# A hybrid gMLP / state-space layer on one core: block sums moved ahead, dt's place among the gates, layer norm of v behind the scan

## Chip, core and metric

The kernel runs on one core of a Trainium2 chip. Five engines run side by side, each through its own queue of instructions in order: TensorE (PE, matmuls and transposes), VectorE (DVE), ScalarE (ACT), GpSimd (POOL) and SyncE (SP, which here only issues DMAs). The metric is the device time of one execution in microseconds. The kernel before took 2279.49 us in the median of three runs (2277.6 to 2282.93).

## The reference

One layer (DEPTH is 1) works on T = 1024 prompt tokens and 64 sample tokens of width 1024, all in fp32. Cut to what matters:

```
h = rms_norm(x, pre_mix_w)
u, v, z, xbc, dt_raw, g_a, g_b = split(h @ w_in)          # 1024 -> u 1024, v 1024, z 2048, xbc 3072, dt 32, gates 2 x 1024
u = gelu(u)
v = layer_norm(gelu(v), gmlp_ln_w, gmlp_ln_b)             # v of the sample rows is an output
o_a = u * gmlp_spatial(v, gmlp_ws, gmlp_bs)               # per group a 128 x 128 mix over positions
xbc, conv_state = causal_conv(xbc, ...)                   # width 4, silu
dt = softplus(dt_raw + dt_bias);  a = -exp(a_log)
y, h_last = ssd(xs, dt, a, B, C, h0)                      # state-space scan, 4 groups of 8 heads
o_b = gated_group_rms_norm(y + d_skip * xs, z, ssm_norm_w)
x = x + rms_norm((sigmoid(g_a) * (o_a @ w_branch_a) + sigmoid(g_b) * (o_b @ w_branch_b)) @ w_out)
x = x + rms_norm(relu(rms_norm(x) @ w_up)^2 @ w_down)
```

## The kernel before

Tokens lie in tiles: tiles 0 to 7 are prompt rows of 128, tile 8 holds the 64 sample rows. Every fp32 matrix is split into a high and a low part (ACT writes the high part, line 81; DVE or POOL subtracts for the low one, line 82), and a product takes three matmuls: high by high, low by high, high by low. A weight block is loaded into a buffer "raw", of which there are two in the whole kernel, and split from there into "wh" and "wl".

A scheduler puts the instructions of each engine into an order from the program, with its own estimate of when each can start; at run time an engine takes them in that order. A buffer of a pool can be written again when its last reader is done, and a pool that opens over the space of a closed one waits in the same way.

The stages around the change, in program order:

1. *z, lower columns.* h is normalised tile by tile, transposed and split (first, first_T). Two halves of z's lower 1024 columns follow, each with four weight quarters (wM, lines 102 to 110) and a loop over the nine tiles (z_tile). Beside the second half, sums() makes block sums of h (operands e4, e5, e6) on POOL and DVE.
2. *v and z's upper columns by seven products.* Each is a 2 x 2 block product with seven products instead of eight, in the order P2, P1, P6, P5, P7, P3, P4, first for v (b = 0), then for z (b = 1). build() (line 352) loads weight pieces and adds them up on POOL for the product after next, prep() splits them for the next one. The pool "pm" of this stage opens over the space of stage 1. sum_e1 (line 481) makes one more block sum, E1, four times: two additions on POOL, a subtraction on DVE and a split. In the loop over products these four are popped from a list at every odd m, from the first product on.
3. *gates.* gate_gen (line 570) is a generator of 48 projections of 24 matmuls; each next() does one. Three stand before the scan's pool "ssd" opens, 5 behind the scan and 4 behind u; the others lie inside the scan.
4. *dt, scan operands and scan.* dt_part (line 199) is a generator: dt's weights and matmuls, then the softplus chain on DVE and ACT, then two cumulative sums on PE (lines 254 and 257) and their transposes. For each of four groups (gi) the operands B, C and x are projected, passed through the convolution (xbc_chunk) and the scan runs tile by tile (stage_a, stage_b, stage_c) on three big buffers "xs" of 128 x 1536.
5. *Layer norm of v.* v_d holds gelu(v) in DRAM. ln_gen (line 656) normalises it tile by tile in place: load two halves, sum, centre, square, scale, store. It is stepped once for each third of a projection of x, and twice behind each group's scan; it has two half buffers "ln".
6. *u and the spatial mix*, then o_a @ w_branch_a with the gates, and what follows. The transposes of the norm's weight and bias (lnr, line 876) stand ahead of the first spatial mix.

The layer norm's step in the projection loop and the rest of it are:

```
                for q in range(4):
                    for t, th in xbc_chunk(gi * 4 + q, lambda t: sp.tile([P, 384], F32, tag="th", bufs=3, name="th")):
                        next(lng, None)
                        ...
            for _ in range(5):
                next(gates)
            for _ in lng:
                pass
```

Of the kernel before, what the change touches and what calls it, by code (L numbers as in the profile page):

```python
# [8 lines left out]
F32 = mybir.dt.float32  # L9
# [6 lines left out]
P = 128  # L16
D = 1024
# [29 lines left out]
def program(tc, a):  # L47
# [3 lines left out]
    with ctx:  # L51
# [32 lines left out]
        def wunit(src, shape, lo_eng=None, pool=None):  # L84
# [3 lines left out]
            raw = wpool.tile([P, 1024], F32, tag="raw", bufs=2, name="raw")  # L88
# [13 lines left out]
        def wM_gen(w, c0, lo_eng=None, pool=None):  # L102

            pool = pool or [None] * 4
            for j in range(4):
                src = w[j * 256:(j + 1) * 256, c0:c0 + 512].rearrange("(k p) n -> p k n", p=P)
                yield wunit(src, (2, 512), lo_eng, pool[j])
# [244 lines left out]
        def build(k, q):  # L352
# [4 lines left out]
            base = k > 1  # L357
# [33 lines left out]
        with tc.tile_pool(name="p0", bufs=1, side="right") as p0:  # L391
# [81 lines left out]

        with tc.tile_pool(name="pm", bufs=1, side="right") as pm, tc.tile_pool(name="xp1", bufs=3, space=PSUM) as xp:
# [31 lines left out]
            for k, (b, n) in enumerate(plan):  # L506
# [12 lines left out]
                for m in range(4):  # L519
# [61 lines left out]
        for _ in range(3):  # L581
            next(gates)
        first_w = [wT(w_in, OFF_X + (16 + gi) * P) for gi in range(1)]
        u_w = []
        with tc.tile_pool(name="ssd", bufs=1, side="right") as sp, \
# [11 lines left out]
            tp = tpp.tile([P, 4, P], F32, tag="tp", name="tp")  # L597
            pe.transpose(tp[:, 0, :120], crow[:120, 0, :], ident[:120, :120])
            pe.transpose(tp[:, 1, :72], crow[:72, 1, :], ident[:72, :72])
            v.tensor_scalar(out=cw, in0=tp[:, 0, :120], scalar1=0.5, scalar2=None, op0=ALU.mult)  # L600
            v.tensor_copy(hist.rearrange("p w c -> p (w c)"), tp[:, 1, :72])

# [53 lines left out]
            def ln_gen():  # L656

                def half(name):
                    return sp.tile([P, 512], F32, tag="ln", bufs=2, name=name)

                for i in (8, 0, 1, 2, 3, 4, 5, 6, 7):
                    R = ROWS[i]
                    hs_ = [half("la"), half("lb")]
                    for f in range(2):
                        nc.sync.dma_start(out=hs_[f][:R], in_=v_d[i * P:i * P + R, f * 512:f * 512 + 512])
                    yield
                    m = sp.tile([P, 8], F32, tag="lm", bufs=2, name="lm")
                    for f in range(2):
                        v.tensor_reduce(out=m[:R, f:f + 1], in_=hs_[f][:R], axis=mybir.AxisListType.X, op=ALU.add)
                    g.tensor_tensor(out=m[:R, 2:3], in0=m[:R, 0:1], in1=m[:R, 1:2], op=ALU.add)  # L670
                    g.tensor_scalar(out=m[:R, 2:3], in0=m[:R, 2:3], scalar1=-1.0 / D, scalar2=None, op0=ALU.mult)
                    yield
                    for f in range(2):
                        s.activation(hs_[f][:R], hs_[f][:R], AF.Identity, bias=m[:R, 2:3])
                    yield
                    jk = sp.tile([P, 4, P], F32, tag="s4", bufs=1, name="jk").rearrange("p a b -> p (a b)")
                    for f in range(2):
                        s.activation(jk[:R], hs_[f][:R], AF.Square, accum_out=m[:R, 3 + f:4 + f])
                    g.tensor_tensor(out=m[:R, 5:6], in0=m[:R, 3:4], in1=m[:R, 4:5], op=ALU.add)
                    r = rsq(sp, m[:, 5:6], R, D, 4 * EPS)  # L680
                    yield
                    for f in range(2):
                        v.tensor_scalar(out=hs_[f][:R], in0=hs_[f][:R], scalar1=r[:R], scalar2=None, op0=ALU.mult)
                        nc.sync.dma_start(out=v_d[i * P:i * P + R, f * 512:f * 512 + 512], in_=hs_[f][:R])
                    if i == 8:
                        yield
                        for f in range(2):
                            x = hs_[f]
                            o = sp.tile([P, 4, P], F32, tag="s4", bufs=1, name="lo").rearrange("p a b -> p (a b)")
                            for name, op in (("gmlp_ln_w", ALU.mult), ("gmlp_ln_b", ALU.add)):  # L690
                                nc.sync.dma_start(out=o[:R], in_=a[name][0, f * 512:f * 512 + 512].partition_broadcast(R))
                                v.tensor_tensor(out=x[:R], in0=x[:R], in1=o[:R], op=op)
                            g.dma_start(out=a["new_gmlp_v_sample"][0, 0][:, f * 512:f * 512 + 512], in_=x[:R])
                        yield
# [3 lines left out]
            dtg = dt_part(wa, wb_, wc, wd)  # L698
            next(dtg)
# [901 lines left out]
```

## Time and profile before

| what | number |
|---|---|
| median of three runs | 2279.49 us |
| the profiled execution | 2282.59 us, of which the span from first to last instruction is 2280.5 |
| PE busy with matmuls | 2173.4 us, 95% of the span |
| PE weight loads, beside matmuls | 1954.6 us, 86% |
| DVE, ACT, POOL busy | 1426.2 (63%), 967.3 (42%), 901.0 us (40%) |
| mean granted clock of TensorE | 0.982 of full speed |

PE is the engine that sets the time: in 40 slices of the span it is below 90% in only a few, most of them early. Matmuls are pipelined, so a listed duration is longer than the step from one to the next. A row of a timeline reads: start and duration in us, engine, line, operation, output and inputs, shape and count, and in brackets the idle time of that engine before it and what ended it. SPq, ACTq and POOLq are DMA issues. A row of windows reads: the stretch, its length in us, then the busy time (and count) of PE, PE's weight loads, DVE, ACT and POOL, the granted clock as a share of full speed, the share of the DMA engines' time and GB/s; its sum row adds the windows up (546 to 609, 711 to 771, and the two that are shown).

### The profile page before, as it was taken

The page shows a single profiled execution, that of the slowest core. Times are in us where ns is not written, and L with a number is a line of the kernel's source. Part 1 is how long each engine was busy: PE and PEld are TensorE (multiplying, and loading weights), DVE is VectorE, ACT ScalarE, POOL GpSimd, SP SyncE. Part 2 cuts the span into 40 slices and gives each one's busy share as a digit, 9 for nine tenths or more (in the row PEclk, how much of TensorE's full clock was granted, in tenths as well). Part 3 has the DMA queues.
Part 4 walks back from the last instruction along what each step waited for, and adds up shares of the span by engine and source line. Part 5 has one row for each costly group of instructions (what it writes and reads, how often), then busy time and mean ns, then how long its engine had stood idle before and what let it go on. Part 6 is the DMA issues. An engine that isn't in the chain of part 4 may idle for free.

```text
span 2280.5 us, 33458 instructions
## 1 busy us (share of the span) xinstructions
PE 2173.4 (95%) x12547; PEld 1954.6 (86%) x12547; DVE 1426.2 (63%) x1972; ACT 967.3 (42%) x1875; POOL 901.0 (40%) x861
## 2 busy tenths in 40 slices
PE   8979997999999999999999999998999998999997
PEld 6767777978889879989999999777999997788785
DVE  5667646676677676665732247377555556577777
ACT  5225435446455545433321123245555554433333
POOL 3455521374473572662221455353222223122134
PEclk9999998999999999999999999999999999999999
DMA  6245662153344352342253535443445457534543
GB/s 206 87 130 190 191 191 77 53 148 109 116 140 123 99 137 75 109 141 75 79 189 91 168 114 170 148 155 117 146 152 154 130 159 242 162 110 135 171 121 111
DMA packets 332939, 309.15 MB, mean 136 GB/s; under 512 B 41499, under 2 KB 286957, under 8 KB 332265
## 3 DMA queue, kind: packets, MB, share of 16 engines
q1 hardware_dynamic: 300648, 268.77, 39.4%
q10 hardware_dynamic: 27152, 22.29, 2.9%
q0 software_dynamic: 4976, 15.95, 1.9%
q8 instruction: 99, 1.62, 0.3%
q14 instruction: 64, 0.52, 0.1%
HBM read 224.68 MB, written 81.49 MB: 134 GB/s over the span
## 4 chain that ended last, share of the span: by engine, by line
PE 64%; DVE 9%; POOL 8%; DMA 8%; issue 8%; ACT 3%; SPq 0%; ACTq 0%; POOLq 0%; DVEq 0%
PE ps L120 7%; PE ps L119 7%; PE ps L121 7%; PE X L1233 3%; PE X L1231 3%; PE X L1232 3%; PE X L1382 3%; PE X L1383 3%; PE X L1381 2%; PE ps L1381 2%; PE ps L1382 2%; PE ps L1383 2%; PE ps L971 2%; PE ps L970 2%; PE ps L969 2%
## 5 line engine op out<-in xcount | busy, mean ns | idle before, releaser
L119 PE MATMUL ps<-hTh,wh 128*128 128x384 f32 (+1 forms) x1152 | 387.0, 336 | 0.0
L120 PE MATMUL ps<-hTl,wh 128*128 128x384 f32 (+1 forms) x1152 | 385.3, 334 | 0.0
L121 PE MATMUL ps<-hTh,wl 128*128 128x384 f32 (+1 forms) x1152 | 384.7, 334 | 0.0
L82 POOL TENSOR_TENSOR wl<-raw,wh 128x1024 fp32r<-128x1024 f32 x74 | 181.9, 2460 | 249.7 <-ACT wh L81 241.2
L81 ACT ACTIVATE wh<-raw 128x1024 fp32r<-128x1024 f32 x112 | 118.4, 1057 | 254.6 <-PE ps L120 98.5
L120 PEld LDWEIGHTS ps<-hTl,wh 128*128 128x128 f32 x1152 | 217.6, 189 | 8.8 <-issue 8.1
L119 PEld LDWEIGHTS ps<-hTh,wh 128*128 128x128 f32 x1152 | 217.6, 189 | 8.0 <-issue 7.4
L121 PEld LDWEIGHTS ps<-hTh,wl 128*128 128x128 f32 x1152 | 217.5, 189 | 6.4 <-issue 6.3
L1231 PE MATMUL X<-hb,wu 128*128 128x272 f32 x512 | 147.9, 290 | 1.5 <-ACT ev L1238 1.0
L627 DVE SCALAR_TENSOR_TENSOR acc<-raw,cw,acc 128x384 f32<-128x384 f32 (+1 forms) x216 | 132.8, 616 | 25.1 <-ACT acc L625 20.6
L1232 PE MATMUL X<-hb,wu 128*128 128x272 f32 x512 | 147.7, 289 | 0.0
L1233 PE MATMUL X<-hb,wu 128*128 128x272 f32 x512 | 146.4, 290 | 0.0
L1375 POOL TENSOR_TENSOR wd<-wd,wd 128x1024 f32<-128x1024 f32 x32 | 85.4, 2672 | 113.2 <-DVE dl L82 74.8
L759 ACT ACTIVATE bc<-bc,pcum 128x128 f32<-128x128 f32 (+1 forms) x288 | 90.6, 384 | 85.9 <-POOL bc L756 83.4
L970 PE MATMUL ps<-ob,wh 128*128 128x384 f32 (+1 forms) x384 | 125.4, 327 | 0.0
L971 PE MATMUL ps<-ob,wl 128*128 128x384 f32 (+1 forms) x384 | 125.4, 327 | 0.0
L969 PE MATMUL ps<-ob,wh 128*128 128x384 f32 (+1 forms) x384 | 125.4, 326 | 0.0
L81 ACT ACTIVATE dh<-wd 128x1024 fp32r<-128x1024 f32 x56 | 59.1, 1055 | 153.6 <-PE ps L1382 79.6
L82 DVE TENSOR_TENSOR dl<-xd,dh 128x1024 fp32r<-128x1024 f32 x56 | 100.5, 1820 | 4.0 <-DMA rs_d<-C 2.5
L82 DVE TENSOR_TENSOR dl<-wd,dh 128x1024 fp32r<-128x1024 f32 x56 | 72.0, 1292 | 48.9 <-ACT dh L81 47.2
L1382 PE MATMUL X<-dl,dh 128*128 128x512 f32 x256 | 100.4, 395 | 0.0
L1383 PE MATMUL X<-dh,dl 128*128 128x512 f32 x256 | 100.3, 394 | 0.0
(447 smaller groups left out, 6047.4 us busy)
## 6 DMA issues: line engine op xcount, KB each, us to landing
raw<-w_in SPq DMA_DIRECT2D x56, 512.0 KB, 4.0
xd<-rc_d SPq DMA_DIRECT2D x112, 256.0 KB, 4.0
rc_d<-E SPq DMA_DIRECT2D x32, 544.0 KB, 3.5
bc<-ac_d SPq DMA_DIRECT2D x64, 256.0 KB, 4.0
raw<-w_branch_b SPq DMA_DIRECT2D x32, 512.0 KB, 3.8
wr<-w_up SPq DMA_DIRECT2D x32, 512.0 KB, 4.1
wd<-w_down SPq DMA_DIRECT2D x16, 1024.0 KB, 5.8
w<-w_in SPq DMA_DIRECT2D x28, 512.0 KB, 4.1
```

What stands on the lines that cost most here:

```text
L81: s.activation(hi, src, AF.Copy)
L82: (lo_eng or v).tensor_tensor(out=lo, in0=src, in1=hi, op=ALU.subtract)
L119: pe.matmul(ps[:, :n], wh[:, k, :], hh[:, k, :n], start=(k == 0), stop=False)
L120: pe.matmul(ps[:, :n], wh[:, k, :], hl[:, k, :n], start=False, stop=False)
L121: pe.matmul(ps[:, :n], wl[:, k, :], hh[:, k, :n], start=False, stop=(k == 7))
L969: pe.matmul(ps[:, :n], wh[:, k, :], ob[:, kk, :], start=(k == 0), stop=False)
L970: pe.matmul(ps[:, :n], wh[:, k, :], ob[:, 4 + kk, :], start=False, stop=False)
L1231: pe.matmul(ps, wh[:, k, :], bh[:, k, :], start=start and k == 0, stop=False, skip_group_check=chain)
L1232: pe.matmul(ps, wh[:, k, :], bl[:, k, :], start=False, stop=False, skip_group_check=chain)
L1233: pe.matmul(ps, wl[:, k, :], bh[:, k, :], start=False, stop=k == 3, skip_group_check=chain)
L1382: pe.matmul(ps, xh, wl, start=False, stop=False, skip_group_check=chain)
L1383: pe.matmul(ps, xl, wh, start=False, stop=q == 3, skip_group_check=chain)
```

## The change

It has four parts.

- *z, second half:* two of the four weight quarters are loaded into two "xt" buffers of stage 1 instead of the two "raw" ones, and the sample tile goes first in the loop over tiles.
- *E1 and the pieces of w11:* for P1, as before for the later products, the pieces come into buffers "k4" of the pool "pm" instead of "raw". The second addition of E1 goes from POOL to DVE, and the four steps are popped at P1's m = 3 and P6's m = 0, 1, 2.
- *dt:* one gate projection, dt's matmuls, one gate, the rest of dt's softplus, one gate, and then the transposes of the convolution's weights, instead of three gates, those transposes and dt. In the loop over B's projection dt's generator is stepped at the last third only.
- *Layer norm of v:* ln_gen handles one whole tile, in one of the three "xs" buffers, and runs behind the last scan, three tiles at a time, with the nine remaining gates between; none are left behind u.

```diff
-            ws = wM(w_in, OFF_Z + 512, pool=[(p0, 1)] + [None] * 3)
+            ws = wM(w_in, OFF_Z + 512, pool=[(p0, 1)] + [None] * 3, raws=[None] * 2 + [lambda: p0.tile([P, D], F32, tag="xt", bufs=2, name="raw")] * 2)
...
-            for i in range(NT):
+            for i in (8, 0, 1, 2, 3, 4, 5, 6, 7):
                 z_tile(ws, 1, i)
...
-            base = k > 1
+            base = k > 0
...
-                for x, i in ((x12, 4 + m), (x11, m)):
-                    g.tensor_tensor(out=x, in0=row_op(i, 0, 0), in1=row_op(i, 0, 1), op=ALU.add)
+                for x, i, e in ((x12, 4 + m, g), (x11, m, v)):
+                    e.tensor_tensor(out=x, in0=row_op(i, 0, 0), in1=row_op(i, 0, 1), op=ALU.add)
...
-                        if todo:
-                            todo.pop(0)()
+                    if todo and (k == 1 and m == 3 or k == 2 and m < 3):
+                        todo.pop(0)()
...
-        for _ in range(3):
-            next(gates)
...
+            def ln_gen(i):
+
+                R = ROWS[i]
+                w = sp.tile([P, 3, 512], F32, tag="xs", bufs=3, name="lnw").rearrange("p a b -> p (a b)")
+                x, jk = w[:R, 0:D], w[:R, D:D + 512]
+                nc.sync.dma_start(out=x, in_=v_d[i * P:i * P + R, :])
...
+                yield
+                yield
+                m = sp.tile([P, 8], F32, tag="lm", bufs=4, name="lm")
+                v.tensor_reduce(out=m[:R, 0:1], in_=x, axis=mybir.AxisListType.X, op=ALU.add)
+                g.tensor_scalar(out=m[:R, 2:3], in0=m[:R, 0:1], scalar1=-1.0 / D, scalar2=None, op0=ALU.mult)
+                yield
+                s.activation(x, x, AF.Identity, bias=m[:R, 2:3])
+                yield
+                for f in range(2):
+                    s.activation(jk, x[:, f * 512:f * 512 + 512], AF.Square, accum_out=m[:R, 3 + f:4 + f])
+                g.tensor_tensor(out=m[:R, 5:6], in0=m[:R, 3:4], in1=m[:R, 4:5], op=ALU.add)
+                r = rsq(sp, m[:, 5:6], R, D, 4 * EPS)
+                yield
+                v.tensor_scalar(out=x, in0=x, scalar1=r[:R], scalar2=None, op0=ALU.mult)
+                nc.sync.dma_start(out=v_d[i * P:i * P + R, :], in_=x)
...
+            next(gates)
             next(dtg)
-            lng = ln_gen()
+            next(gates)
+            next(dtg)
+            next(gates)
...
-                    next(dtg, None)
+                    if t == 2:
+                        next(dtg, None)
...
-                        next(lng, None)
...
-                next(lng, None)
-                next(lng, None)
-            for _ in range(5):
-                next(gates)
-            for _ in lng:
-                pass
+
+            live, left = [], [ln_gen(i) for i in (8, 0, 1, 2, 3, 4, 5, 6, 7)]
+            turn = 0
+            while live or left:
+                while left and len(live) < 3:
+                    live.append(left.pop(0))
+                live = [x for x in live if next(x, True) is None]
+                turn += 1
+                if turn % 2 == 0:
+                    next(gates, None)
```

POOL's order at the start of stage 2, before. Lines 365 and 367 add up P6's two weight pieces (v2, one of each line per piece), line 485 makes E1's block sums, line 316 is part of v's gelu, line 321 a store.

```order
L316 TENSOR_SCALAR t_1118<-t_1118 128x512
L367 TENSOR_TENSOR v2_1030<-v2_1030,w12_1035 128x1024
L316 TENSOR_SCALAR t_1150<-t_1150 128x512
L485 TENSOR_TENSOR x_1088<-hTh1_96,hTl1_97 128x512
L485 TENSOR_TENSOR x_1087<-hTh0_94,hTl0_95 128x512
L321 DMA v_d_81<-cz_1015 128x512
L365 TENSOR_TENSOR v2_1079<-v2_1079,w11_1081 128x1024
L485 TENSOR_TENSOR x_1143<-hTh2_98,hTl2_99 128x512
L321 DMA v_d_81<-cz_1045 128x512
L485 TENSOR_TENSOR x_1142<-hTh0_94,hTl0_95 128x512
```

In this piece the second weight piece, v2_1079, has only its first addition. The same place with the change:

```order
L431 DMA z_d_80<-sz_962 128x512
L365 TENSOR_TENSOR v2_1030<-v2_1030,w11_1032 128x1024
L367 TENSOR_TENSOR v2_1030<-v2_1030,w12_1035 128x1024
L485 TENSOR_TENSOR x_1178<-hTh1_96,hTl1_97 128x512
L365 TENSOR_TENSOR v2_1072<-v2_1072,w11_1074 128x1024
L367 TENSOR_TENSOR v2_1072<-v2_1072,w12_1077 128x1024
L316 TENSOR_SCALAR t_1104<-t_1104 128x512
L316 TENSOR_SCALAR t_1129<-t_1129 128x512
```

Both pieces now stand directly behind z's last store (line 431), with one block sum between them.

SP's order of DMA issues around the load of the norm's weights (lnr), before. raw is a weight load, sz a tile of z and bc a block of decays for the scan, bs belongs to the spatial mix, vc is the first reload of the normalised v.

```order
L746 DMA sz_9156<-z_d_80 128x512
L755 DMA bc_9268<-ac_d_83 128x4x128
L746 DMA sz_9254<-z_d_80 128x512
L90 DMA raw_10021<-w_in 128x8x128
L90 DMA raw_10167<-w_in 128x8x128
L870 DMA lnr_9617<-gmlp_ln_w 8x128
L871 DMA lnr_9617<-gmlp_ln_b 8x128
L185 DMA bs_9724<-gmlp_bs 128x128
```

And with the change (lines 653 and 673 are the norm's loads and stores, each name lnw_... one tile):

```order
L673 DMA v_d_81<-lnw_9354 128x1024
L673 DMA v_d_81<-lnw_9401 128x1024
L653 DMA lnw_9489<-v_d_81 128x1024
L673 DMA v_d_81<-lnw_9487 128x1024
L653 DMA lnw_9533<-v_d_81 128x1024
L90 DMA raw_10503<-w_in 128x8x128
L673 DMA v_d_81<-lnw_9489 128x1024
L673 DMA v_d_81<-lnw_9533 128x1024
L871 DMA lnr_9661<-gmlp_ln_w 8x128
L872 DMA lnr_9661<-gmlp_ln_b 8x128
L185 DMA bs_9768<-gmlp_bs 128x128
```

These are the norm's last four tiles (4 to 7; the store of tile 3 opens the piece, that of tile 4 is the second row). The load of tile 7, lnw_9533, follows the store of tile 4, lnw_9401, whose buffer it takes; the load of the norm's weights follows the last tile's store.

## Rows read from the trace of the kernel before

**Rows 1.** PE's timeline, second half of z (start, us, engine, line, operation)

```profile
75.59 0.50 PE L134 MATMUL ps<-wl,hTh 128*128 128x512 f32 x1 [3.09 <-DVE wl L82]
...
78.27 0.63 PE L135 MATMUL ps<-wh,hTl 128*128 128x512 f32 x1
...
80.74 0.39 PE L133 MATMUL ps<-wh,hTh 128*128 128x512 f32 x1
...
92.58 0.50 PE L133 MATMUL ps<-wh,hTh 128*128 128x512 f32 x1 [1.88 <-DVE sz L430]
```

**Rows 2.** PE's timeline, product P6 of v

```profile
158.41 0.80 PE L493 MATMUL X<-wh,e4h 128*128 128x512 f32 x1 [3.67 <-DVE cz L532]
...
172.83 2.07 PE L493 MATMUL X<-wh,e4h 128*128 128x512 f32 x4 [9.95 <-ACT wh L81]
```

**Rows 3.** POOL's timeline, P6's weight pieces and block sums

```profile
141.46 2.40 POOL L365 TENSOR_TENSOR v<-v,w 128x1024 f32<-128x1024 f32 x1 [1.24 <-DMA v<-w_in]
...
157.85 2.96 POOL L485 TENSOR_TENSOR x<-hTh,hTl 128x512 f32<-128x512 f32 x2
...
163.47 2.79 POOL L367 TENSOR_TENSOR v<-v,w 128x1024 f32<-128x1024 f32 x1
```

**Rows 4.** Timelines of SP and PE, dt's weights, matmuls and cumulative sum

```profile
323.04 0.34 SPq L185 DMA_DIRECT2D dskip<-d_skip  x1
...
325.69 0.43 SPq L213 DMA_DIRECT2D wd<-w_in  x1
...
330.39 0.36 PE L219 MATMUL ps<-hTh,wd 128*32 128x384 f32 x1 [2.41 <-ACT wd L81]
...
369.35 1.30 PE L254 MATMUL ps<-wb__2427,wa 128*128 128x288 f32 x2 [14.14 <-DVE wb__2427 L250]
```

**Rows 5.** Windows: projections without the norm, scan's end to u's end, sum of four

```profile
872.00:936.00 64.00, 64.00 (x405) 63.51 (x404) 42.71 (x76) 33.18 (x74) 14.59 (x18) 1.00 0.21 56
1018.00:1156.00 138.00, 138.00 (x878) 136.16 (x877) 85.14 (x165) 46.11 (x88) 36.80 (x36) 1.00 0.32 92
sum 325.00, PE 319.59 PEld 314.69 DVE 214.18 ACT 153.59 POOL 91.29; mean PE 79.90 PEld 78.67 DVE 53.55 ACT 38.40 POOL 22.82
```

**Rows 6.** E1's sums by their tile: ns min/median/max, first and last start

```profile
L486 DVE TENSOR_TENSOR x<-x x4: 693/1132/4273, 140.2 to 166.7; 128x512 f32<-128x512 f32 x4
```

**Rows 7.** Timelines of POOL and PE, scan's end

```profile
1011.01 1.29 POOL L796 TENSOR_TENSOR y<-y,xs 128x512 f32<-128x512 f32 x1 [2.06 <-DVE y L795]
...
1017.55 0.60 PE L650 MATMUL tp<-ident,S 128*128 128x128 f32 x4
...
1032.03 0.23 PE L876 MATMUL tp<-ident,lnr 16*128 16x16 f32 x1
```

**Rows 8.** DMA issues: count, KB each, median us to landing

```profile
la<-v_d SPq DMA_DIRECT2D x6, 256.0 KB, 2.7
...
v_d<-la SPq DMA_DIRECT2D x7, 256.0 KB, 2.1
...
vc<-v_d SPq DMA_DIRECT2D x8, 512.0 KB, 4.2
```

**Rows 9.** Lines, layer norm: busy us, mean ns of one | idle before

```profile
L143 POOL TENSOR_TENSOR rs<-rs,pw 128x1 f32<-128x1 f32 (+1 forms) x45 | 27.0, 601 | 2.7
...
L674 ACT ACTIVATE la<-la,lm 128x512 f32<-128x512 f32 (+1 forms) x9 | 6.5, 721 | 19.4 <-POOL lm L671 17.8 <-POOL raw L611 1.6
...
L669 DVE TENSOR_REDUCE lm<-la 128x1 f32<-128x512 f32 (+1 forms) x9 | 6.2, 685 | 12.7 <-DMA la<-v_d 12.7
...
L678 ACT ACTIVATE jk<-la 128x512 f32<-128x512 f32 (+1 forms) x9 | 5.6, 623 | 0.6 <-DMA new_ssm_prompt<-s 0.6
...
L683 DVE TENSOR_SCALAR la<-la,rs 128x512 f32<-128x512 f32 (+1 forms) x9 | 4.4, 488 | 8.0 <-POOL rs L143 8.0
```

**Rows 10.** SP's timeline, one tile of the layer norm

```profile
716.13 0.46 SPq L665 DMA_DIRECT2D la<-v_d  x1
...
732.74 0.32 SPq L684 DMA_DIRECT2D v_d<-la  x1
```

More of the change, by code (lines that the diff above doesn't have):

```diff
@@ L82, in split, with wunit @@
             (lo_eng or v).tensor_tensor(out=lo, in0=src, in1=hi, op=ALU.subtract)
-        def wunit(src, shape, lo_eng=None, pool=None):
+        def wunit(src, shape, lo_eng=None, pool=None, raw=None):
             pool, nb = pool or (wpool, 4)
             m = shape[0] * shape[1]
-            raw = wpool.tile([P, 1024], F32, tag="raw", bufs=2, name="raw")
+            raw = raw() if raw else wpool.tile([P, 1024], F32, tag="raw", bufs=2, name="raw")
             r3 = raw[:, :m].rearrange("p (a b) -> p a b", a=shape[0])
@@ L100, in wT, with wM_gen @@
             return wunit(src, (8, P), lo_eng)
-        def wM_gen(w, c0, lo_eng=None, pool=None):
-            pool = pool or [None] * 4
+        def wM_gen(w, c0, lo_eng=None, pool=None, raws=None):
+            pool, raws = pool or [None] * 4, raws or [None] * 4
             for j in range(4):
                 src = w[j * 256:(j + 1) * 256, c0:c0 + 512].rearrange("(k p) n -> p k n", p=P)
-                yield wunit(src, (2, 512), lo_eng, pool[j])
+                yield wunit(src, (2, 512), lo_eng, pool[j], raws[j])
         def wM(*args, **kw):
@@ L596, in program @@
             nc.sync.dma_start(out=crow[0:72, 1, :], in_=a["cache_conv"][0, 0].rearrange("w (c p) -> (w c) p", p=P))
[L597 to L601, printed above, removed]
             def xbc_chunk(c, out):
@@ L654, in hbc @@
                 return x.unsqueeze(2).to_broadcast([R, HG, HD])
[L656 to L665, printed above, removed]
-                    yield
[L667 to L671, printed above, removed]
-                    yield
[L673 to L694, printed above, removed]
@@ new lines, in ln_gen @@
+            def ln_gen(i):
[3 more added lines that the diff above has]
+                nc.sync.dma_start(out=x, in_=v_d[i * P:i * P + R, :])
+                if i == 8:
+                    wb8 = sp.tile([P, 3, 512], F32, tag="xs", bufs=3, name="lnb")[:R]
+                    names = [("gmlp_ln_w", 0), ("gmlp_ln_b", 0), ("gmlp_ln_w", 1), ("gmlp_ln_b", 1)]
+                    for k, (name, f) in enumerate(names[:3]):
+                        nc.sync.dma_start(out=wb8[:, k, :], in_=a[name][0, f * 512:f * 512 + 512].partition_broadcast(R))
+                yield
[13 more added lines that the diff above has]
+                nc.sync.dma_start(out=v_d[i * P:i * P + R, :], in_=x)
+                if i == 8:
+                    nc.sync.dma_start(out=jk, in_=a["gmlp_ln_b"][0, 512:1024].partition_broadcast(R))
+                    yield
+                    yield
+                    for k, (name, f) in enumerate(names):
+                        xf = x[:, f * 512:f * 512 + 512]
+                        v.tensor_tensor(out=xf, in0=xf, in1=wb8[:, k, :] if k < 3 else jk, op=ALU.mult if k % 2 == 0 else ALU.add)
+                    g.dma_start(out=a["new_gmlp_v_sample"][0, 0], in_=x)
@@ L698, in program @@
             dtg = dt_part(wa, wb_, wc, wd)
+            next(gates)
             next(dtg)
-            lng = ln_gen()
+            next(gates)
+            next(dtg)
+            next(gates)
+            tp = tpp.tile([P, 4, P], F32, tag="tp", name="tp")
+            pe.transpose(tp[:, 0, :120], crow[:120, 0, :], ident[:120, :120])
+            pe.transpose(tp[:, 1, :72], crow[:72, 1, :], ident[:72, :72])
+            v.tensor_scalar(out=cw, in0=tp[:, 0, :120], scalar1=0.5, scalar2=None, op0=ALU.mult)
+            v.tensor_copy(hist.rearrange("p w c -> p (w c)"), tp[:, 1, :72])
             for gi in range(G):
```

## The prediction

> **What bounds the kernel now.** I read the page first. By its first part, in the table above, PE has matmuls running for 2173 of 2280.5 us, so only the 107 us in which it runs nothing, and the stretches in which it runs at half speed, are to be had. The change adds and drops next to no matmuls. Everything is therefore a question of where PE waits, and I went through PE's waits from the longest down and asked of each whether the change touches it; the timeline of PE gave their places. In the second half of z's projection PE waits 3.09 us for a weight split and 1.88 us for a finished z tile, and after each the matmuls run at half speed for a while (0.63 us long where they are 0.39 later) [rows 1]. In product P6 it waits 3.67 and 9.95 us [rows 2], the second time for weights that POOL has to add up first: POOL's pieces of that weight begin at 141.46 and end at 166.26, with block sums between them [rows 3]. At dt it waits 2.41 us for dt's weights and 14.14 us for the softplus chain [rows 4]. In the projections of the scan's first operands PE is idle 5.4 us over the two windows in which the layer norm runs beside them (the sum of the four windows less their two gapless rows), and not at all in the window without it; nor from the scan's end to the end of u [rows 5]. The waits inside the scan, some 16 us in all, are not touched.
>
> **The change part by part.** The sum is made against the profiled execution, 2282.59 us, which lies 3.1 us above the median of the runs, 2279.49.
>
> *z, second half.* Two of four weight quarters get buffers of their own and are loaded early, and the block sums no longer stand on DVE ahead of the splits. That takes the 3.09 and the 1.88 us and two half-speed stretches of eight matmuls each, 16 x 0.24 = 3.8: 8.8 at most. Nothing else is queued between the splits, but the sums now all lie in this half, with their DVE and POOL work (block adds, splits) beside z's. Bounds 0 to 8.8; I take 6, near the upper end, since only the engine order could give it back.
>
> *P6.* In the new order POOL's two weight pieces follow the opening with one block add between them instead of six and some gelu work: 2 x 2.4 + 2 x 2.8 + 1.5, about 12 us from the first load's arrival, where it took 24.8 [rows 3]. PE needs them 26 us after z's end and has them after 22 to 26. Also the buffers of this block come free behind the last prompt tile of z, not behind the sample tile (which now goes first), so the block's loads go out some 6 us sooner. Gone: 3.67 + 9.95 idle [rows 2] and twenty half-speed matmuls, 4.8: 18.4 at most. What is late next: P1's pieces of w11 now use a buffer of the new block and cannot be loaded before it opens; they are split some 12 us after z's end, when PE wants them. Bounds 5 to 18.4, value 15. By the Trainium skill (SBUF — State Buffer, "Who interferes with whom") a DVE instruction with two SBUF inputs and a GpSimd instruction that reads SBUF exclude each other, so a block add moved from POOL to DVE would still hold POOL up; the four DVE subtractions beside POOL's adds took 0.69 to 4.27 us here, which agrees [rows 6]. By that rule the term would be some 2 us smaller.
>
> *dt.* One gate projection instead of three stands ahead of dt's matmuls. 82 PE instructions between the scan's end and the transposes of the norm's weights took 13.9 us, 0.169 each [rows 7]; 48 matmuls fewer and the two transposes moved bring PE to dt 8.5 us sooner. But dt's weights are loaded by SP behind the constant that waits for the last z writes (323.04, then 325.69) [rows 4], and no part of the change moves that. So PE stands 2.41 + 8.5 = 10.9 us, and runs at half speed for some 1.8 us worth after it. The 14.14 us go: two gates, B's three projections and one of C now lie between, 120 matmuls or 20 us, and DVE has no norm work in between. Before, 2.41 + 14.14 + 1.8 = 18.4; now 12.7. Gain 5.7, bounds 0 (the chain still late) to 18.4 (the weights in time); value 5.
>
> *Layer norm out of the projections.* 5.4 us idle [rows 5] and one half-speed stretch, 1.9. Bounds 0 to 7.3; value 6, as the window without the norm has no gap.
>
> *Layer norm behind the scan: the loss.* The norm's tiles now use the scan's three big buffers and pass through them in turn; the first load of the steady chain can go out when the scan's last addition has read its operand, at 1011.01 + 1.29 = 1012.3 [rows 7]. Tiles 0, 1, 4 and 7 share one buffer, and each must be stored before the next is loaded: four rounds in a row. A round: load of 512 KB, 4.2 as for vc [rows 8]; reduction over 1024, 2 x 0.69; centring 2 x 0.72; squares 2 x 0.8 with their accumulator read; scaling 2 x 0.49; four small POOL operations of 0.3 to 0.6 us, 1.8 together [rows 9]; the store, 2.1 for half the bytes [rows 8], scaled as the loads are (4.2 to 2.7) to 3.3. That is 14.7, four rounds 58.8, end at 1071.1. Meanwhile PE has, from the scan's end at 1018.15, 110 gate matmuls, two transposes and the 72 of u's first weight column: 184 x 0.169 = 31.1, to 1049.3. There it stops, because the transposes of the norm's weights come next, whose load stands on SP behind the last store, and because u's next projection needs a PSUM buffer that u's gelu must empty, which stands on ACT behind the last tile's squares. With 2.5 us for that gelu PE starts again at 1073.6: 24.3 idle, 26 with the half speed after it. Before it had none there [rows 5]. Bounds: at the landing times of the half-size transfers (2.7 and 2.1) a round is 12 and the cost 14; if a round takes as long as the old one, 716.13 to 732.74 from load to store issue [rows 10] and 2.1 for the store, 18.7, the cost is 40 and 42 with half speed. I take 26: the sum of the durations is nearer to what a free queue gives.
> The Trainium skill (DMA: Bandwidth & Descriptors, "Anatomy of one DMA") gives a transfer a fixed 2.0 us and 1 us for each 436 KB, by which 512 KB is an estimated 3.2 us both ways; the 4.2 of vc is above it. By the page the rounds would be 13.6 and the cost 22. Its rule to start a load early and wait for it late speaks against this part of the change: here each load starts only when the buffer's last store has landed.
>
> *End of u.* Four gate projections that followed u are used up earlier: 96 x 0.169 = 16 us of cover for the last spatial mix, whose v rows take 4.2 us to reload [rows 8] and whose results pass DVE and ACT before PE's next product. Parts of that product are ordered between, so I take 5, bounds 0 to 12.
>
> *Sum.* Gains 6 + 15 + 5 + 6 = 32, losses 26 + 5 = 31: 1 us less than the profiled run, so 2281.6 for it and about 2278 for the median.
>
> **The rivals.** *The norm hides (faster).* Rounds of 12 instead of 14.7 and the gaps of u's end filled: 12 + 5 us less, 2261. For it: DMA is little used there and ACT, DVE and POOL have a third of their time free; against it, SP issues in order, and a store that waits holds the loads behind it. *The norm's rounds stay as long as they were (slower).* One mechanism: each store on SP waits for its tile, and the next loads stand behind it whatever is free; 18.7 a round, 16 us more, 2294. It decides from a round of 16 on. For it: the old cycle of 16.6; against it, that one was stretched by projections' work on all four engines, of which the gates have little. *P6 keeps its stall.* P1's weights, held until the block opens, push P6's behind them: 15 us back, 2293. For it: those loads were free of the opening before; against it, the opening itself comes sooner. *dt's weights come in time*: 12.7 less, 2265; only a change in SP's order could do it, and there is none.
>
> **How the numbers follow.** This kernel's runs can tell no change from 0.2%, 4.6 us. Forecast 0.45, spread over 2270 to 2286 (faster 0.15, same 0.20, slower 0.10). The norm hides 0.24, nearly all faster. Long rounds 0.18 and P6's stall 0.08, nearly all slower, a small part of either near no change. dt in time 0.05. Together faster 0.41, same 0.28, slower 0.31. Leaving out the ends of the rivals, the range is 2259 to 2297.
>
> **What would show it.** z: no gap over 1 us in its second half. P6: POOL's second piece within 13 us of the first, no wait for wh over 4 us. dt: one wait of about 11 us at the first dt matmul and none at the cumulative sum. Projections: no gap beside the first operands. Tail: one PE gap of 20 to 28 us, some 31 us after the scan's end, with four load-store rounds before it. The forecast is wrong if that gap is under 14 or over 40 us, or if dt's is missing.

## The result, and the profile after

The changed kernel took 2296.15 us in the median of four runs (2293.37 to 2297.07), against 2279.22 for the kernel before: a ratio of 1.007, 95% interval 1.0052 to 1.0087. It is slower by about 17 us, well beyond what the runs can tell from no change. The forecast was 2278, no change to speak of. The profiled execution's span is 2295.0 us, 14.5 more than before, and the mean granted clock 0.979.

PE's longest waits in the changed kernel (line, what it waited for, us in total, times, longest):

```profile
PE tp L877 <- DVE gq L195: 27.0, 1, 27.0
PE tp L809 <- DVE y L800: 17.3, 16, 2.0
PE ps L219 <- DMA s<-state_ssm: 10.3, 1, 10.3
PE ps L493 <- DVE c L540: 8.0, 1, 8.0
...
PE ps L133 <- DVE sz L430: 6.2, 1, 6.2
```

The first is the tail behind the scan, the third dt's weights (the releaser named is merely the last event before it), and both are where the prediction put them. The fourth and the last are new: a wait at product P5 and one in z's second half. The waits of [rows 1], [rows 2] and the 14.14 us of [rows 4] are gone.

PE executes the same work in the same order of stages in both kernels, so the start of a stage's first matmul dates what each stage gained or lost. Stage lengths on PE in us: z up to v's first product; the seven products, twice; from the first gate to the last transposed state of the scan; from there to the first matmul of the product with w_out (1440.15 before, 1455.99 after); and the rest of the span.

| kernel | z | products | dt, operands, scan | tail, u, o_a, o_b | rest |
|---|---|---|---|---|---|
| before | 125.6 | 189.8 | 702.5 | 422.3 | 840.3 |
| changed | 124.8 | 183.8 | 690.0 | 457.3 | 839.0 |
| difference | -0.8 | -6.0 | -12.5 | +35.1 | -1.3 |
| forecast | -6 | -15 | -11 | +31 | 0 |

Four gains of 32 us together were forecast and some 19 came; losses of 31 were forecast and 35.1 came. These are lengths in one execution of each kernel. Kernels below that share the code of a stage differ in it by up to 1.8 us in z, 2.8 in the products, 3.7 in dt and scan, 2.3 in the tail and 6 in the rest, so the 0.8 of z is no gain that can be told from none.

**z's second half.** POOL's first block sums, before and with the change:

```profile
45.84 2.54 POOL L439 TENSOR_TENSOR w<-hTh,hTl 128x512 f32<-128x512 f32 x2 [1.40 <-DVE xn L407]
```

```profile
69.83 4.44 POOL L439 TENSOR_TENSOR w<-hTh,hTl 128x512 f32<-128x512 f32 x2 [2.31 <-DVE wl L82]
```

At run time the sums of the kernel before begin beside z's first half; with the change they begin 24 us later. DVE's timeline in the changed kernel, and the wait that it ends on PE:

```profile
99.03 2.91 DVE L443 TENSOR_TENSOR w<-w 128x512 f32<-128x512 f32 x1
101.86 0.68 DVE L82 TENSOR_TENSOR e5l<-w,e5h 128x512 fp32r<-128x512 f32 x1
102.47 1.75 DVE L82 TENSOR_TENSOR e4l<-w,e4h 128x512 fp32r<-128x512 f32 x1
104.14 1.74 DVE L82 TENSOR_TENSOR e6l<-w,e6h 128x512 fp32r<-128x512 f32 x1
105.81 0.68 DVE L430 SCALAR_TENSOR_TENSOR sz<-sz,ps 128x512 f32<-128x512 f32 x1
```

```profile
106.53 0.80 PE L133 MATMUL ps<-wh,hTh 128*128 128x512 f32 x1 [6.17 <-DVE sz L430]
107.13 0.63 PE L134 MATMUL ps<-wl,hTh 128*128 128x512 f32 x1
```

Line 430 empties the PSUM buffer of a z tile. It stands behind the subtractions and splits of the block sums (lines 440 to 443 and 82), which the order now packs between two tiles of this half. Line 443's subtraction, 0.67 to 0.69 us each of the three other times, took 2.91 beside two of POOL's adds (98.86 to 101.38). So a wait of 6.17 us with half speed behind it replaces the 3.09 and the 1.88.

**P5.** ACT's timeline, a row of DVE's, and PE's row:

```profile
170.19 0.64 ACT L81 ACTIVATE hTh<-x 128x512 fp32r<-128x512 f32 x1 [2.49 <-DVE x L486]
...
179.23 0.63 ACT L81 ACTIVATE hTh<-x 128x512 fp32r<-128x512 f32 x1 [4.63 <-DVE x L486]
179.77 1.07 ACT L536 ACTIVATE c<-X 128x512 f32<-128x512 f32 x2
180.72 0.60 ACT L539 ACTIVATE c<-ps 128x512 f32<-128x512 f32 x1
```

```profile
177.46 1.74 DVE L486 TENSOR_TENSOR x<-x 128x512 f32<-128x512 f32 x1
```

```profile
182.10 0.80 PE L493 MATMUL ps<-wh,e5h 128*128 128x512 f32 x1 [8.04 <-DVE c L540]
```

The copies of P6's results out of PSUM (line 536) and of P5's first (line 539) stand on ACT behind E1's splits (line 81), and those wait for E1's subtraction on DVE (line 486), which took 2.90 and 1.74 us here. The step of E1 that was put off reached the engines just when they had P6's results to clear. DVE is the full engine here, ACT mostly waits for it; a window of this stretch:

```profile
150.00:187.00 37.00, 27.17 (x109) 20.73 (x108) 35.78 (x32) 16.16 (x25) 23.92 (x17) 0.91 0.54 162
```

**The tail.** SP's timeline of the norm (653 loads, 673 stores), then ACT's first gelu and PE's return:

```profile
991.46 0.34 SPq L653 DMA_DIRECT2D lnw<-v_d  x1
...
1005.91 4.07 SPq L653 DMA_DIRECT2D lnw<-v_d  x3
...
1022.34 0.32 SPq L653 DMA_DIRECT2D lnw<-v_d  x1
...
1039.01 0.32 SPq L673 DMA_DIRECT2D v_d<-lnw  x1
1039.43 0.37 SPq L653 DMA_DIRECT2D lnw<-v_d  x1
...
1047.65 3.39 SPq L673 DMA_DIRECT2D v_d<-lnw  x2
1053.46 0.30 SPq L871 DMA_DIRECT2D lnr<-gmlp_ln_w  x1
```

```profile
1053.50 0.87 ACT L193 ACTIVATE gq<-ps 128x384 f32<-128x384 f32 x2 [4.78 <-DMA v_d<-lnw]
```

```profile
1055.82 0.26 PE L877 MATMUL tp<-ident,lnr 16*128 16x16 f32 x1 [27.01 <-DVE gq L195]
1058.63 0.69 PE L119 MATMUL ps<-hTh,wh 128*128 128x384 f32 x1 [2.56 <-DVE gh L866]
```

The loads of tiles 0, 1, 4 and 7 went out at 991.46, about 1006, 1022.34 and 1039.43: rounds of 14.5, 16.4 and 17.1, where 14.7 were forecast. The loads landed after 5.4 us in the median where 4.2 were counted (and 3.2 by the prediction's other estimate), the stores after 2.9 where 3.3 were counted. PE had no work for 27.0 us where [rows 5] show none idle, and 2.6 more behind it. ACT's row says what holds u's gelu: not the norm's squares ahead of it on ACT, as the prediction had it, but the landing of the norm's last store, for which ACT stands idle 4.78 us. That fits the pool of u's buffers, which opens over the scan's; the load of the norm's weights goes out at the same moment.

The DMA engines, little used by the prediction's account, are nearly full in this stretch. Two windows of it; the second last number is the DMA engines' share:

```profile
999.00:1012.00 13.00, 13.00 (x80) 13.00 (x79) 5.07 (x7) 3.51 (x7) 4.99 (x7) 1.00 0.96 304
...
1020.00:1030.00 10.00, 8.80 (x55) 8.54 (x53) 3.03 (x5) 2.03 (x5) 5.35 (x8) 1.00 0.97 321
```

In the kernel before that share was 0.32 behind the scan [rows 5].

At the end of u PE waits once for 3.26 and once for 0.85 us in o_a's product:

```profile
1190.38 0.41 PE L119 MATMUL ps<-oah,wh 128*128 128x320 f32 x1 [3.26 <-DVE mg L953]
...
1203.35 0.42 PE L119 MATMUL ps<-oah,wh 128*128 128x320 f32 x1 [0.85 <-DVE mg L953]
```

### The profile page after: what moved, and what is told of

Same layout as the page of the kernel before. It is cut to its first block, busy times and chain, and to the rows that moved or that the text cites. A ratio compares the mean times of both kernels' runs of the same rounds, so it can differ in the third digit from the quotient of the medians.

```text
span 2295.0 us, 33408 instructions
## 1 busy us (share of the span) xinstructions
PE 2169.6 (95%) x12547; PEld 1951.4 (85%) x12547; DVE 1432.9 (62%) x1958; ACT 963.9 (42%) x1866; POOL 889.3 (39%) x847
## 4 chain that ended last, share of the span: by engine, by line
PE 67%; DVE 8%; DMA 8%; POOL 7%; issue 6%; ACT 4%; SPq 1%; ACTq 0%; POOLq 0%; DVEq 0%
PE ps L120 7%; PE ps L119 7%; PE ps L121 7%; PE X L1234 3%; PE X L1232 3%; PE X L1233 3%; PE X L1383 3%; PE X L1384 3%; PE X L1382 2%; PE ps L1384 2%; PE ps L1382 2%; PE ps L1383 2%; DMA bc<-ac_d 2%; PE ps L972 1%; PE ps L971 1%
```

## The experiments

Each kernel ran beside the kernel before on the same chip, which took 2280 to 2283.5 us there; kernels of different chips are best compared by their ratios. The stage lengths as above (the rest of the span is 839 to 845 in all):

| kernel | z | products | dt, operands, scan | tail to o_b | median | ratio to before, interval |
|---|---|---|---|---|---|---|
| changed, norm as before | 125.0 | 186.3 | 699.2 | 422.3 | 2276.95 | 0.9984 (0.9970 to 0.9999) |
| changed, z as before | 124.3 | 187.9 | 686.3 | 458.2 | 2300.66 | 1.0088 (1.0070 to 1.0107) |
| changed, E1 and w11 as before | 125.2 | 184.3 | 688.6 | 459.6 | 2299.18 | 1.0078 (1.0058 to 1.0098) |
| before, norm moved | 126.5 | 188.9 | 685.9 | 457.3 | 2302.98 | 1.0102 (1.0087 to 1.0118) |
| norm as before, E1 spread | 125.2 | 193.0 | 699.7 | 422.3 | 2284.31 | 1.0014 (1.0002 to 1.0026) |
| norm as before, z weights in raw | 123.5 | 186.1 | 698.4 | 422.4 | 2277.76 | 0.9984 (0.9971 to 0.9997) |
| norm as before, dt's weights early | 126.5 | 186.6 | 683.2 | 422.3 | 2260.68 | 0.9909 (0.9889 to 0.9929) |
| changed, fourth buffer | 125.7 | 184.5 | 687.8 | 457.6 | 2297.95 | 1.0076 (1.0059 to 1.0092) |
| changed, fourth buffer, stores on POOL | 126.6 | 184.8 | 688.1 | 453.5 | 2293.30 | 1.0057 (1.0040 to 1.0074) |
| three edits | 122.6 | 188.3 | 681.4 | 422.2 | 2257.53 | 0.9884 (0.9866 to 0.9902) |
| three edits, norm from group 1 on | 122.4 | 187.6 | 689.9 | 422.3 | 2268.71 | 0.9936 (0.9916 to 0.9955) |
| three edits, norm in the scan's loop | 122.4 | 186.0 | 687.1 | 422.9 | 2260.12 | 0.9901 (0.9883 to 0.9919) |

**One part undone or alone.** First the norm put back:

```diff
-            live, left = [], [ln_gen(i) for i in (8, 0, 1, 2, 3, 4, 5, 6, 7)]
...
+                        next(lng, None)
...
+            for _ in range(5):
+                next(gates)
+            for _ in lng:
+                pass
```

> The changed kernel with the layer norm of v put back into the projections and nine gates as before (5 behind the scan, 4 behind u); z, E1 and dt as changed. Theory A (the move of the norm is what costs: 27 + 2.6 us idle and half speed at the tail, 5 us at the end of u, against 6 us gained in the projections): 2296 - 36 + 6 = 2266, no PE gap over 2 us between the scan's end and o_a's product. Rival B (the other parts give nothing, since each shifts its wait to the next place): 2276 to 2280.

The tail is back at 422.3, to 0.1 us that of the kernel before: the 35.1 us are the norm's and its gates' alone. The kernel is 19 us faster than the changed one, not 30: the middle stage loses 9.2 instead of 6, and 5.8 more lie in the products and the rest, whose code is the same in both. The mechanism of A was met for the tail, where PE has no gap over 0.3 us. The number is B's, and so is what it means: z's part, E1's and dt's order, forecast at 26 us together, make the kernel without the norm's move 0.16% faster than before, some 4 us.

Then z's part undone (against the changed kernel), E1's and w11's part undone, and the norm's move alone, which is the last part of the change's diff put into the kernel before:

```diff
-            ws = wM(..., raws=[None] * 2 + [lambda: p0.tile([P, D], F32, tag="xt", bufs=2, name="raw")] * 2)
+            ws = wM(...)
-            for i in (8, 0, 1, 2, 3, 4, 5, 6, 7):
+            for i in range(NT):
```

```diff
-            base = k > 0
+            base = k > 1
-                    e.tensor_tensor(out=x, in0=row_op(i, 0, 0), in1=row_op(i, 0, 1), op=ALU.add)
+                    g.tensor_tensor(out=x, in0=row_op(i, 0, 0), in1=row_op(i, 0, 1), op=ALU.add)
-                    if todo and (k == 1 and m == 3 or k == 2 and m < 3):
-                        todo.pop(0)()
+                        if todo:
+                            todo.pop(0)()
```

> The changed kernel with z's second half as before (weights through the two raw buffers, tiles 0 to 8 in order). Theory A (the z part trades a 3.1 and a 1.9 us wait for one of 6.2): 2297, and the 6.2 us wait for z's tile is gone or short. Rival B (the tile order also brings the opening of the next block forward): 6 us more, 2302, with a wait for P6's weights back.

> The changed kernel with E1's sums and P1's w11 pieces as before. Theory A (that part gains 6 us: 18 at P6 less 12 at P5, where E1's late steps stand ahead of the copies of P6's results): 2302, wait of about 10 us at P6 and none of 8 at P5. Rival B (the wait at P6 goes by the earlier opening of the block alone): 2290 or less.

> The kernel before with the move of the layer norm alone. Theory A: 2279 + 36 - 6 = 2309, with one PE gap of 25 to 30 us behind the scan. Rival B (the tail gap comes about only because dt and E1 let PE arrive earlier): 2290, gap under 15.

Without z's part z is no longer, as A said, and the products are 187.9, against 183.8 to 186.6 in the five executions with both parts; the wait for P6's weights does not come back, as B had it. Without E1's part the products are 184.3, within those five, and the long wait at P6 does not come back either, against A; the 2299 is not B's number. PE's waits of that kernel there:

```profile
PE ps L493 <- DVE c L540: 3.2, 1, 3.2
...
PE X L494 <- DVE wl L82: 2.2, 1, 2.2
```

So the wait of [rows 2] has two remedies, z's part (its tile order, as the best version below shows) or E1's edits, and either takes it away; with both, the second adds between nothing and 4. The wait of 8 us at P5, too, is there only with both: 3.2 without E1's part, 1.7 without z's. The norm's move alone costs 23 us, 7 less than A's sum: its tail is the same 35, but it gains 16.6 in the middle stage, not 6. PE's waits of that kernel show why:

```profile
PE tp L874 <- DVE gq L195: 26.6, 1, 26.6
...
PE X L493 <- ACT wh L81: 9.8, 1, 9.8
...
PE ps L254 <- DVE wb__2427 L250: 6.8, 1, 6.8
```

The 14.14 us of [rows 4] fall to 6.8 by the norm's absence from DVE alone, with dt's order as before. Adding dt's new order then gains nothing: 685.9 without it, 686.3 to 690.0 in the five executions with it. With the norm in place the new order gains about 3 (702.5 to 699.2). The two parts removed the same wait, and the new order of dt pays 10 us at dt's weights for it.

**E1's steps spread.** This kernel and the next two are edits of the changed kernel with the norm as before.

```diff
-                    if todo and (k == 1 and m == 3 or k == 2 and m < 3):
+                    if todo and (k in (2, 3) and m % 2 == 1):
                         todo.pop(0)()
```

> The changed kernel with the layer norm as before the change (which took 2277), and E1's four steps spread over P6 and P5 (at odd m) instead of P1's last and P6's first three. Theory A (E1's steps stand on ACT and DVE ahead of the copies of P6's results and hold P5): the wait of 8 us at P5 falls under 2, 2268. Rival B (P5 waits for weights or POOL then): another wait of 5 to 8 us there or at P7, 2277.

B in its mechanism, worse than its number: the wait at P5 falls from 8 to 1.1, and others come around it.

```profile
175.76 0.70 PE L493 MATMUL X<-wh,hTh 128*128 128x512 f32 x1 [3.41 <-ACT wh L81]
177.73 0.79 PE L494 MATMUL X<-wl,hTh 128*128 128x512 f32 x1 [1.27 <-DVE wl L82]
180.07 0.80 PE L493 MATMUL ps<-wh,e5h 128*128 128x512 f32 x1 [1.12 <-DVE c L540]
```

Another of 8.5 us follows at z's P6, for the result of its P1. The products take 193.0, more than before the change. DVE is still busy for 34.3 of the 37 us from 150 to 187, ACT for 16.2; in this trial, moving E1 moved the wait. That DVE's load is the reason for the new wait is likely, not shown.

**z's weights in raw, tile order kept.**

```diff
-            ws = wM(..., pool=[(p0, 1)] + [None] * 3, raws=[None] * 2 + [lambda: p0.tile([P, D], F32, tag="xt", bufs=2, name="raw")] * 2)
+            ws = wM(..., pool=[(p0, 1)] + [None] * 3)
```

> The changed kernel with the layer norm as before the change (2277), and z's last two weight quarters through the two raw buffers again; the sample tile still first. Theory A (the quarters in the xt buffers keep the block sums, which need the same buffers, out of z's first half; bunched in the second they hold z's tile): the 6.0 us wait for z's tile goes, one of about 3 for a weight split comes back, 2273 to 2275. Rival B (the tile order bunches the sums): the 6 us wait stays, 2277 or more.

A in its mechanism: the first block sum is back at 45.86, the 6 us wait is gone, one of 3.73 for a weight split is there, and z takes 123.5 against 124.8 to 126.6. The extra load buffers for z were taken from the block sums. The time is B's 2277 or more: a gain of 1 to 3 us is lost in the spread of the runs.

**dt's weights in the weight pool.**

```diff
+        wd = [wpool.tile([P, 1024], d_, tag=tg, bufs=nb, name="wd")[:, 0:8 * H].rearrange("p (k n) -> p k n", k=8)
+              for d_, tg, nb in ((F32, "raw", 2), (F32R, "wh", 4), (F32R, "wl", 4))]
+        nc.sync.dma_start(out=wd[0], in_=w_in[:, OFF_DT:OFF_DT + H].rearrange("(k p) n -> p k n", p=P))
+        split(*wd)
         first_w = [wT(w_in, OFF_X + (16 + gi) * P) for gi in range(1)]
         with tc.tile_pool(name="ssd", bufs=1, side="right") as sp, \
...
-            wd = [sp.tile([P, 4, P], dt, tag="bc", bufs=4, name="wd") for dt in (F32, F32R, F32R)]
```

> The changed kernel with the layer norm as before the change (2277), and dt's weights loaded and split in buffers of the weight pool, ahead of the scan's pool. Theory A (dt's weights come late because their buffers are in a pool that opens behind z's last stores): the 11 us wait at dt's first matmul and its half speed go, 2265. Rival B (the softplus chain or the convolution's weights, which still wait for the pool, take its place): a wait of 8 or more behind dt, 2275 or more.

A, and more: 16 us. The load of dt's weights and dt's first matmul, without this edit and with it:

```profile
321.47 0.43 SPq L213 DMA_DIRECT2D wd<-w_in  x1
...
326.80 0.53 PE L219 MATMUL ps<-hTh,wd 128*32 128x384 f32 x1 [11.12 <-DMA la<-v_d]
```

```profile
264.84 0.37 SPq L581 DMA_DIRECT2D wd<-w_in  x1
...
313.48 0.34 PE L217 MATMUL ps<-hTh,wd 128*32 128x384 f32 x1
```

The 11.1 us wait is gone, and so is one of 4.4 behind dt, for B's convolution, that the kernel without this edit had. Alone dt's new order gained about 3 us, with this edit 19; early weights with the old order were not run.

**The tail's buffers and stores.** A fourth buffer; then a fourth buffer with the stores on POOL's queue:

```diff
+                if i in (0, 3, 6):
+                    x = sp.tile([P, D], F32, tag="lx", bufs=1, name="lx")[:R]
...
-                while left and len(live) < 3:
+                while left and len(live) < 4:
```

```diff
-                w = sp.tile([P, 3, 512], F32, tag="xs", bufs=3, name="lnw").rearrange("p a b -> p (a b)")
+                tg, nb = ("lx", 1) if i in (0, 2, 6) else ("xs", 3)
+                w = sp.tile([P, 3, 512], F32, tag=tg, bufs=nb, name="lnw").rearrange("p a b -> p (a b)")
...
-                nc.sync.dma_start(out=v_d[i * P:i * P + R, :], in_=x)
+                g.dma_start(out=v_d[i * P:i * P + R, :], in_=x)
...
-                while left and len(live) < 3:
+                while left and len(live) < 4:
```

> The changed kernel with one more buffer of 128 x 1024 for the norm behind the scan (tiles 0, 3 and 6 pass through it, their squares' scratch is the scan's s4 buffer), four tiles live. Theory A (four load-to-store rounds in a row through one buffer set the tail): three rounds now, the gap ahead of the norm's weight transposes falls from 27 to about 13, 2282. Rival B (the norm's work on ACT, DVE and POOL and SP's order set it, whatever the buffers): gap over 22, 2291 or more.

> The changed kernel with a fourth buffer of 128 x 1536 for the norm (tiles 0, 2 and 6 pass through it), four tiles live, and the norm's stores issued on POOL's queue, so that no load stands behind a store on SP. Theory A (three rounds in a row; in the trial before, SP held the third load behind two stores): the gap ahead of the norm's weight transposes falls from 27 to under 17, 2285. Rival B (a round is as long as its slowest engine's queue lets it, and POOL, which now waits for each scaling, holds the next tile): gap over 22, 2292 or more.

B in both. The gaps:

```profile
PE tp L881 <- DMA lnr<-gmlp_ln_b: 25.8, 1, 25.8
```

```profile
PE tp L878 <- DMA bs<-gmlp_bs: 23.5, 1, 23.5
```

In the first, tile 6's load stood on SP behind two stores, though its buffer's store had gone out at 1029.55 and landed at 1032.28; that is 2.7 us of it:

```profile
1029.55 0.32 SPq L677 DMA_DIRECT2D v_d<-lx  x1
1031.02 3.85 SPq L677 DMA_DIRECT2D v_d<-lnw  x2
1034.97 0.38 SPq L657 DMA_DIRECT2D lx<-v_d  x1
```

With the stores off SP the loads behind the scan went out in bunches of three, one and two, and the next thing was late: three loads issued from 1005.12 ended the waits of their reductions at 1011.15, 1013.71 and 1015.20, with the DMA engines busy for 96% of the 10 us from 1005, and two scalings (3.49 and 2.82 us) stretched beside POOL's weight splits:

```profile
1011.15 1.22 DVE L663 TENSOR_REDUCE lm<-lnw 128x1 f32<-128x1024 f32 x1 [5.56 <-DMA lnw<-v_d]
1013.71 1.22 DVE L663 TENSOR_REDUCE lm<-lnw 128x1 f32<-128x1024 f32 x1 [1.34 <-DMA lnw<-v_d]
1015.20 1.22 DVE L663 TENSOR_REDUCE lm<-lnw 128x1 f32<-128x1024 f32 x1 [0.27 <-DMA lnw<-v_d]
...
1039.68 2.82 DVE L673 TENSOR_SCALAR lnw<-lnw,rs 128x1024 f32<-128x1024 f32 x1 [4.34 <-POOL rs L143]
```

So the number of rounds through one buffer, by which I had worked out the tail, does not set it alone: from the scan's end to the landing of the last store it is 54 us with three buffers, 53 with four, and 49 with four and the stores off SP, and PE has some 30 us of work for that time. What is left is SP's order, the small operations on POOL with the scalings beside its splits, and the full DMA engines. Which of these is the hardest stays open; no run lightened the DMA engines' load.

**The best version**, made of three small edits to the kernel before: the sample tile first in z's second half, dt's new order, dt's weights in the weight pool (the last two as in the diffs above).

```diff
-            for i in range(NT):
+            for i in (8, 0, 1, 2, 3, 4, 5, 6, 7):
                 z_tile(ws, 1, i)
```

> The kernel before with three small edits: the sample tile first in z's second half, the changed kernel's order of dt and gates, and dt's weights in buffers of the weight pool; weights of z, E1, w11 and the layer norm as before. Theory A (the long wait at P6 goes by the earlier opening of the block, which the tile order alone brings; E1's and w11's edits add nothing): no wait over 4 us at P6 or P5, first gate 309 or earlier, 2258. Rival B (E1's edits are what takes it away): the wait of about 10 us at P6 is there, 2268 to 2272.

A in its mechanism and its time: 2257.5 us, 1.2% under before. No wait at P6 or P5 is over 3.2 us, with E1, w11 and z's buffers as they were. The first gate starts at 310.9, not 309; in the two kernels below, whose code is the same up to there, at 310.0 and 308.4. With all of z's and E1's parts it is 308.7 to 313.0 in five executions, and 315.4 in the kernel before: the one line of tile order brings what those two parts bring. Two more kernels move the norm on top of these edits, one out of the first group's projections, one into the scan's loop:

```diff
-                        next(lng, None)
+                        if gi:
+                            next(lng, None)
```

```diff
-                        next(lng, None)
...
                     if k >= 2:
                         stage_c(order[k - 2])
+                    next(lng, None)
```

> The same with the layer norm's steps left out of the first group's projections, so that it starts beside the second group's; steps that remain run behind the scan. Theory A (the norm costs in the projections it stands beside by DVE time, and in the first group by standing in the softplus chain): 2 to 4 us off, 2255. Rival B (dt's chain has slack now, and the steps move to the other groups with their cost): the same as the kernel with the three edits.

> The kernel with the three edits, and the layer norm's steps taken from the projections into the loop of the scan (one at each of its eleven steps), with its two half buffers. Theory A (the norm costs 6 to 8 us beside the projections, and the scan's waits are by POOL's and ACT's chain, which it lengthens by about as much): within 4 us of the kernel with the three edits. Rival B (the scan hides it): 6 to 8 us faster, 2251. Rival C (it delays y's normalisation, on which PE waits in each scan step): 10 us slower.

Neither helps. Started one group later, the norm costs 8.5 us more in that stage, as none of the theories had it. PE's waits for the convolved operands rise (and those for y's normalisation from 14.4 to 18.0); first the kernel with three edits, then this one:

```profile
PE tp L633 <- DVE th L625: 6.9, 6, 2.2
```

```profile
PE tp L633 <- DVE th L625: 14.2, 12, 2.4
```

In the kernel with three edits PE waits 0.4 us for an operand of the first group and never for one of the fourth's; in this one the norm's steps stand beside the fourth group's projections, and there PE waits 2.1, 0.6 and 1.6. In the scan's loop the norm costs 5.7 in that stage, 3 in all, as A had it.

## Why the prediction was wrong, step by step

The step that failed is the one behind each removed wait in the products and in z: the prediction credited the wait and priced next to nothing for the place where the moved work lands. The profiled executions differ by 14.5 us where 1 us the other way was forecast. Of these 15.5 us, 9.0 are missing at P6 and 5.2 in z, and the losses were 4.1 larger; dt and the norm gave 1.5 more than forecast, the rest 1.3.

- *z, second half, 6 us.* Failed: 0.8, no gain that can be told from none. "Only the engine order could give it back", and it did. I saw that the sums all lie in this half and priced nothing for them; seven DVE instructions ahead of one z tile's line 430 cost 6.2 us. With the weights in raw again the wait is gone.
- *P6, 15 us.* The largest failed step: 6.0, and 2 to 6 over five executions. Both waits of [rows 2] went, as forecast, and POOL's pieces came in time. But E1's four steps had to go somewhere, and I asked only whether they still held POOL, not what stands behind them on ACT and DVE at P5, where 8.0 us came back. "What is late next" was put at P1's w11 pieces, which cost nothing. That E1's edits are needed at all was wrong too: the tile order alone does it.
- *dt, 5 us, and the norm out of the projections, 6.* Together 12.5 for 11, near by luck, since the split was wrong. Both were credited from different waits; in fact the norm's instructions were part of the 14.14 us, so its move gains 16.6 alone and dt's order then nothing. The wait for dt's weights, 10.9 forecast, is 10.3. (The two gates, B's three projections and one of C are 144 matmuls and 24 us, not 120 and 20; no term hangs on it.)
- *The tail, 26 us.* Right in place, order and sign, 4 to 5 too small: 27.0 + 2.6 idle and the half speed behind them, 31 of the 35. The sum of rounds was near by luck: another buffer does not shorten it, the loads took longer than counted and the stores less, and the DMA engines, taken as little used, were 96% busy in 23 of the 30 us of work that PE had left.
- *End of u, 5 us.* 4.1 us idle in o_a's product.
- *Rivals.* "The norm's rounds stay as long as they were" came nearest in its mechanism: rounds of 16.4 and 17.1 behind a first of 14.5, against 16 as its point of decision. That its 2294 lies near the measured 2296 is luck: it adds 16 us to the tail, and the tail was 4 to 5 over the forecast; the rest are the missing gains. It was right in the engine it named for a part only, since SP freed of stores changes 4 us. "P6 keeps its stall" has a near time, 2293, in the same way: the stall went, and P5's came.
- *The form of the sum.* Three of the four gains were taken near their upper ends (6 of 8.8, 15 of 18.4, 6 of 7.3), because each removed wait was seen and what its work does elsewhere was not. With the middle of every pair of bounds the same sum gives 5 us slower than before, 2284: 29 gained, 34 lost.

## What to carry to other kernels

Work that is moved takes its queue place with it: for each moved instruction, read on every engine that it uses what stands behind it at the new place, and price that, before crediting the wait that goes. Two edits that each remove a wait may remove the same one; ask of each with the other in place. When a late load is the first thing on the path, look at which pool its buffer is in and what that pool waits for: loading dt's weights into another pool's buffer, and so before that pool opens, gained 16 us in the kernel with dt's new order, more than any reordering here.

## What the runs showed of the hardware

- DVE subtractions with two SBUF operands of 128 x 512 took 0.68 us alone and up to 2.91 beside POOL's adds in the same stretch of the changed kernel; the other way round, one of POOL's adds took 4.01 us, 1.28 elsewhere, while DVE's subtractions beside it took 0.67. Scalings of 128 x 1024 took 0.75, and 2.82 beside a weight split on POOL. The Trainium skill (SBUF — State Buffer, "Who interferes with whom") has one exclusive pair of ports shared by the two engines, and the trace agrees.
- The norm's loads of 512 KB landed in 3.8 to 5.8 us in the changed kernel. With the stores on POOL's queue, three issued together released their readers after 6 to 8 us, while the DMA engines were 96% busy at 333 GB/s.
- One gap of 27 us cost no more half speed than a short one: the granted clock, at 0.5 (1.2 GHz) when PE came back, was at 1.0 (2.4 GHz) again 3.9 us after u's matmuls began at 1058.63; behind the 6.17 us wait in z it was 3.6 us after PE's return at 106.53.
